# Sliding-window attention of the prompt: the value product as fp32r matmuls on high and low parts

## The chip, the cores and the metric

The kernel runs on one core of a Trainium2 chip. The metric is the device time of one execution in microseconds; before the change it is 1694.12 us, the median of three runs (1693.13 to 1695.23).

Five engines of the core run their own in-order instruction streams: TensorE (PE in the profile; its weight loads are shown apart as PEld), VectorE (DVE), ScalarE (ACT), GpSimd (POOL) and SyncE (SP), whose queue starts most of the DMA transfers here. Matmuls read SBUF and write PSUM; PSUM is then read out by DVE or ACT.

## The reference

One inference step of a two-layer decoder for a prompt of 512 tokens and 8 samples of 4 tokens, all in fp32. The change touches one piece of the first layer, the attention of the prompt over a sliding window of 128 tokens, with 16 query heads that share 4 key and value heads (4 queries to one):

```python
def gqa_attend(q, k, v, mask=None, bias=None, sink=None):
    s = jnp.einsum('...qkgd,...skd->...kgqs', q, k) * (q.shape[-1] ** -0.5)
    s = jnp.where(mask, s, NEG_INF)
    p = jax.nn.softmax(jnp.concatenate([s, sk], axis=-1), axis=-1)[..., :-1]   # sk: one sink logit per head
    return jnp.einsum('...kgqs,...skd->...qkgd', p, v)

def swa_prompt(q, k, v, sink):
    # blocks of 128 queries; each sees its own block of keys and the one before it
    o = gqa_attend(qb, with_prev(kb), with_prev(vb), mask=mask[:, None, None], sink=sink)
```

The last line of `gqa_attend` is the value product: probabilities times values.

## The kernel before

The step is one long program. Nearly all of PE's time goes to linear layers: weights arrive in pieces of 128 x 1024 numbers (`wpiece`, L154), are split by ACT into a high part that fp32r holds exactly (L162) and by DVE into the rest (L163), and each product is three fp32r matmuls, high x high, high x low, low x high (`acc3`, L180). A piece serves 48 matmuls of 256 or 288 columns. The raw weights have two buffers and the split ones three, so a DMA of a piece waits for the split two pieces earlier, and that split for the matmuls of the piece three before it.

In the first layer (`even`, L614) the program computes keys and values, four pieces of the query projection, and then runs the attention of the prompt beside the linear layers that don't depend on it: four more query pieces (L667), eight pieces of the gate `z` (L669) and twelve pieces of the convolution's input (`conv`, L723). The attention is written inside `with self.ahead(m0)` (L670), which gives it a priority as if it stood ahead of those layers. The order of every engine's stream is then worked out by a scheduler when the program is built: it fills each gap of the attention with linear matmuls. On the chip each engine runs its stream as it stands.

`swa_prompt` (L484) handles one half of the heads (`m`), a block of 128 queries (`c`), and in it two key heads (`r`) with two pairs of query heads (`i`). For one pair: scores on PE from split queries and keys into PSUM (`sc`, two buffers), a maximum on DVE (L502), exponentials on ACT (L507), the reciprocal of the sum on DVE (L510), the scaling on POOL (L513), transposes on PE (L515, by `tr`, L141) into PSUM (`tp`, two buffers), and a copy of them into the tile `PT` (L516, on DVE for the first pair and ACT for the second). When all four pairs of a block are in `PT`, the value product follows (L517 to L523): one key block (`kb`) and one key head (`r`) at a time, a stationary operand of 64 columns (the values) and 512 streamed columns (the four heads' probabilities), both in fp32. The two key heads write the two halves of one PSUM tile `pv` (one buffer); DVE copies it over the queries that it replaces (L523). All matmuls are issued in the helper `mm` at L138.

`swa_sample` (L562) follows, the same attention for the samples; its cached keys and values come by DMA into tiles `skT` and `svc` (L568, L569). Working tiles of 2176 columns (`H`, L122), among them `PT`, `skT`, `svc` and the halves of the queries, share one pool of 13 buffers.

Of the kernel before, what the change touches and what calls it, by code (L numbers as in the profile page):

```python
# [9 lines left out]
F32 = mybir.dt.float32  # L10
F32R = mybir.dt.float32r
# [4 lines left out]
ALU = mybir.AluOpType  # L16
# [3 lines left out]
P = 128  # L20
# [86 lines left out]
class Net:  # L107
# [364 lines left out]
    def stack_q(self, Q, q, m, tok):  # L472
# [7 lines left out]
            nc.vector.tensor_tensor(Q[b, r], src, Q[a, r].bitcast(F32), ALU.subtract)  # L480
        return Q


    def swa_prompt(self, q, K2, V, m):  # L484
        nc = self.nc
        for c in range(4):
            nk = 1 if c == 0 else 2
            W, k0 = 128 * nk, 128 * max(c - 1, 0)
            tok = slice(128 * c, 128 * c + 128)
            Q = self.stack_q(self.sw.tile([P, 1024], F32R, tag="QS", bufs=2, name=self.nm("QS")), q, m, tok)  # L490
            PT = self.H("PT")[:, 0:2048].rearrange("p (k r i t) -> p k r i t", k=2, r=2, i=4)
            for r in range(2):
                for i in (0, 2):
                    hd = 8 * m + 4 * r + i
                    sc = self.psum("sc", [P, 2, 256])
                    s = sc[:, :, 0:W]
                    self.mm(s, self.identb, self.maskb[:, 256 - W:256].unsqueeze(1).to_broadcast([P, 2, W]), True, False)
                    for e in range(2):
                        for z in range(2):
                            self.mm(sc[:, e, 0:W], Q[:, r, i + e], K2[z][:, m, r, k0:k0 + W], False, e == 1 and z == 1)  # L500
                    mx, nm, den, es, rec = (self.ty(2) for _ in range(5))
                    nc.vector.tensor_reduce(mx, s, AX.X, ALU.max, negate=True)  # L502
                    nc.vector.tensor_tensor(nm, mx, self.nsink[:, hd:hd + 2], ALU.min)
                    nc.vector.tensor_tensor(es, nm, self.par[:, V_SK + hd:V_SK + hd + 2], ALU.add)
                    pr = self.sw.tile([P, 2, 256], F32, tag="P", bufs=3, name=self.nm("pr"))
                    for e in range(2):
                        nc.scalar.activation(pr[:, e, 0:W], sc[:, e, 0:W], AF.Exp, bias=nm[:, e:e + 1], accum_out=den[:, e:e + 1])  # L507
                    nc.scalar.activation(es, es, AF.Exp)
                    nc.vector.tensor_tensor(den, den, es, ALU.add)
                    nc.vector.reciprocal(rec, den)  # L510
                    tp = self.psum("tp", [P, 2, 2, 128])
                    for e in range(2):
                        nc.gpsimd.tensor_scalar(pr[:, e, 0:W], pr[:, e, 0:W], rec[:, e:e + 1], 1.0, ALU.mult, ALU.mult)  # L513
                        for kb in range(nk):
                            self.tr(tp[:, kb, e], pr[:, e, 128 * kb:128 * kb + 128])  # L515
                    (nc.scalar.copy if i else nc.vector.tensor_copy)(PT[:, 0:nk, r, i:i + 2], tp[:, 0:nk])  # L516
            pv = self.psum("pv", [P, 4, 128])  # L517
            for kb in range(nk):
                blk = c - nk + 1 + kb
                for r in range(2):  # L520
                    g = 2 * m + r
                    self.mm(pv[64 * r:64 * r + 64], V[:, blk, 64 * g:64 * g + 64], PT[:, kb, r], kb == 0, kb == nk - 1)
            nc.vector.tensor_copy(q.half(m)[:, :, tok], pv)  # L523

    def sample_q(self, q, Qb):
        nc = self.nc
# [87 lines left out]
    def even(self, st, nxt, fill):  # L614
        nc, tc, I, O = self.nc, self.tc, self.I, self.O
        with ExitStack() as es:
            ev = es.enter_context(tc.tile_pool(name="even", bufs=1))
            kT = ev.tile([P, 2, NT], F32, name="kT")
            V = ev.tile([P, 5, 256], F32, name="V")
# [9 lines left out]
            for i, (o, w) in enumerate(TB):  # L629
                ps = self.psum("tr", [P, 288])  # L630
                for k in range(KD):
                    whi, wlo = wv[k // 4][0][:, k % 4], wv[k // 4][1][:, k % 4]
                    a, b = xh[k][:, o:o + w], xl[k][:, o:o + w]
# [18 lines left out]
            nc.sync.dma_start(O["p_swa_v"], V[:, 3])  # L652
            with tc.tile_pool(name="swa", bufs=1) as self.sw, tc.tile_pool(name="conv", bufs=1) as cv:
                K2 = self.stack_k(kT)
                self.linear(wq, range(4), KD, xh, xl, qe)

                def zevac(n, c, ps):
                    o, N = CH[c]
                    z = zs[n][:, o:o + N]
                    nc.vector.scalar_tensor_tensor(z, ps, 0.125, st["b"][:, o:o + N], ALU.mult, ALU.mult)  # L660
                    t = cv.tile([P, 572], F32, tag="cy", bufs=2, name=self.nm("zt"))[:, 0:N]
                    nc.scalar.activation(t, z, AF.Tanh, scale=4.0)
                    self.last = nc.vector.scalar_tensor_tensor(z, t, 1.0, z, ALU.add, ALU.mult)
                m0 = self.mark()
                self.take(q)
                self.take(zs)
                self.linear(wq, range(4, 8), KD, xh, xl, qe)  # L667
                qlast = self.last
                self.linear(self.pieces(I["we_z"], KD), range(8), KD, xh, xl, zevac)  # L669
                with self.ahead(m0):  # L670
                    self.swa_prompt(q, K2, V, 0)
                    self.swa_prompt(q, K2, V, 1)
                    self.swa_sample(q, kT, V, qlast)
                self.conv(st, xs, BC, craw, cv)
            nc.sync.dma_start(O["conv"], craw)
# [1168 lines left out]
```

## Time and profile before

| | |
|---|---|
| median of three runs | 1694.12 us |
| profiled execution | 1698.67 us, of which 1696.9 us span |
| granted clock of TensorE, mean | 0.99 |
| PE busy | 1645.9 us |
| DVE, ACT, POOL busy | 1184.0, 778.3, 328.3 us |
| DMA | 189.27 MB, 112 GB/s on average |

The profile is of one execution. Busy times are unions over an engine's instructions; matmuls are pipelined, so a busy PE may still be slowed by one matmul that takes long. What a matmul costs is best read from the distance between starts, not from its duration. An instruction in the program may be several in the trace: an fp32 matmul is two rows there.

### The profile page before, as it was taken

The page shows a single profiled execution, that of the slowest core. Times are in us where ns is not written, and L with a number is a line of the kernel's source. Part 1 is how long each engine was busy: PE and PEld are TensorE (multiplying, and loading weights), DVE is VectorE, ACT ScalarE, POOL GpSimd, SP SyncE. Part 2 cuts the span into 40 slices and gives each one's busy share as a digit, 9 for nine tenths or more (in the row PEclk, how much of TensorE's full clock was granted, in tenths as well). Part 3 has the DMA queues.
Part 4 walks back from the last instruction along what each step waited for, and adds up shares of the span by engine and source line. Part 5 has one row for each costly group of instructions (what it writes and reads, how often), then busy time and mean ns, then how long its engine had stood idle before and what let it go on. Part 6 is the DMA issues. An engine that isn't in the chain of part 4 may idle for free.

```text
span 1696.9 us, 32362 instructions
## 1 busy us (share of the span) xinstructions
PE 1645.9 (97%) x12720; PEld 1518.7 (89%) x12720; DVE 1184.0 (70%) x2296; ACT 778.3 (46%) x1603; POOL 328.3 (19%) x510
## 2 busy tenths in 40 slices
PE   6999999998999999999999998998999999999997
PEld 6988899886997999999999996655988999999997
DVE  7667678867766887677766567654567877777663
ACT  5255445344444544444445355544545444444444
POOL 5022312657422310000001203111223100000002
PEclk9999999999999999999999999999999999999999
DMA  5211424126533233232323334554551233223222
GB/s 185 63 55 39 145 82 132 51 91 237 207 100 125 81 113 102 89 103 88 106 75 107 127 116 125 160 174 149 181 178 59 75 113 100 94 100 106 75 68 86
DMA packets 71221, 189.27 MB, mean 112 GB/s; under 512 B 7612, under 2 KB 34012, under 8 KB 63452
## 3 DMA queue, kind: packets, MB, share of 16 engines
q1 hardware_dynamic: 69388, 184.84, 32.9%
q8 instruction: 100, 1.64, 0.4%
q10 hardware_dynamic: 1600, 1.83, 0.4%
q0 software_dynamic: 80, 0.52, 0.1%
q14 instruction: 53, 0.43, 0.1%
HBM read 172.22 MB, written 14.95 MB: 110 GB/s over the span
## 4 chain that ended last, share of the span: by engine, by line
PE 91%; DVE 3%; POOL 2%; ACT 1%; issue 1%; DMA 1%; SPq 0%; DVEq 0%; POOLq 0%; ACTq 0%
PE ps L138 66%; PE ps L1563 22%; PE ps L141 3%; POOL room L425 1%; DMA room<-wo_d 0%; POOL sq L421 0%; DVE split_t L1544 0%; ACT prt L1161 0%; DVE prt L1160 0%; DVE xs L879 0%; ACT split_t L162 0%; DMA mem<-mem 0%; DVE meml L252 0%; DVE x L1730 0%; DMA x<-x 0%
## 5 line engine op out<-in xcount | busy, mean ns | idle before, releaser
L138 PE MATMUL ps<-xh,split_t 128*128 128x288 f32 (+1 forms) x2304 | 463.8, 294 | 13.8 <-ACT split_t L162 11.8
L138 PEld LDWEIGHTS ps<-xh,split_t 128*128 128x128 f32 x2304 | 371.1, 190 | 19.8 <-ACT split_t L162 12.8
L1563 PE MATMUL ps<-xf,split_t 128*128 128x272 f32 x2592 | 348.9, 289 | 3.1 <-DVE split_t L1544 2.1
L138 PE MATMUL ps<-xl,split_t 128*128 128x256 f32 (+1 forms) x1152 | 339.1, 295 | 1.2 <-DVE xl L252 1.0
L1563 PEld LDWEIGHTS ps<-xf,split_t 128*128 128x128 f32 x2592 | 335.0, 188 | 4.4 <-DVE split_t L1544 3.0
L261 POOL TENSOR_TENSOR room<-room,sq 128x256 f32<-128x256 f32 (+1 forms) x96 | 86.4, 904 | 773.4 <-ACT sq L260 771.7
L138 PEld LDWEIGHTS ps<-xl,split_t 128*128 128x128 f32 x1152 | 218.9, 190 | 6.9 <-issue 4.3
L138 PE MATMUL ps<-hh,fs 128*128 128x256 f32 (+1 forms) x1024 | 206.3, 288 | 0.0
L162 ACT CAST split_t<-room 128x1024 fp32r<-128x1024 f32 (+1 forms) x128 | 130.3, 1019 | 156.5 <-PE ps L138 112.3
L163 DVE TENSOR_TENSOR split_t<-room,split_t 128x1024 fp32r<-128x1024 f32 (+1 forms) x128 | 157.0, 1229 | 31.5 <-ACT split_t L162 31.0
L138 PEld LDWEIGHTS ps<-hh,fs 128*128 128x128 f32 x1024 | 164.9, 188 | 0.4 <-ACT fs L1607 0.4
L1544 DVE TENSOR_TENSOR split_t<-fr,split_t 128x1024 fp32r<-128x1024 f32 x108 | 131.7, 1221 | 35.3 <-ACT split_t L1543 35.0
L1543 ACT CAST split_t<-fr 128x1024 fp32r<-128x1024 f32 x108 | 113.4, 1052 | 89.6 <-PE ps L1563 53.4
L138 PE MATMUL ps<-hl,fs 128*128 128x256 f32 (+1 forms) x512 | 147.3, 288 | 0.0
L138 PE MATMUL ps<-oh,split_t 128*128 128x288 f32 (+1 forms) x512 | 105.7, 298 | 1.3 <-ACT oh L246 1.2
L138 PEld LDWEIGHTS ps<-hl,fs 128*128 128x128 f32 x512 | 96.4, 188 | 0.0
L138 PEld LDWEIGHTS ps<-oh,split_t 128*128 128x128 f32 x512 | 83.2, 192 | 8.3 <-issue 5.0
L138 PE MATMUL ps<-ol,split_t 128*128 128x288 f32 (+1 forms) x256 | 77.1, 301 | 0.3 <-DVE ol L249 0.2
L1607 ACT CAST fs<-room 128x512 fp32r<-128x512 f32 x64 | 39.4, 618 | 82.6 <-PE ps L138 68.3
L252 DVE SCALAR_TENSOR_TENSOR xl<-x,room,xh 128x256 fp32r<-128x256 f32 (+1 forms) x96 | 69.6, 755 | 5.6 <-ACT xh L251 5.6
L138 PE MATMUL ps<-hh,split_t 128*128 128x256 f32 (+1 forms) x384 | 73.4, 288 | 0.0
L1620 DVE TENSOR_TENSOR x<-x,ps 128x256 f32<-128x256 f32 (+1 forms) x128 | 54.4, 433 | 26.9 <-PE ps L138 26.7
(423 smaller groups left out, 3091.2 us busy)
## 6 DMA issues: line engine op xcount, KB each, us to landing
fr<-wfi SPq DMA_DIRECT2D x36, 1024.0 KB
room<-wfo SPq DMA_DIRECT2D x64, 256.0 KB
room<-wo_e SPq DMA_DIRECT2D x16, 512.0 KB
xk<-mem_k SPq DMA_DIRECT2D x8, 1024.0 KB
xv<-mem_v SPq DMA_DIRECT2D x8, 1024.0 KB
room<-wfi SPq DMA_DIRECT2D x16, 512.0 KB
fox_k<-fox_k SPq DMA_DIRECT2D x64, 128.0 KB
fox_v<-fox_v SPq DMA_DIRECT2D x64, 128.0 KB
```

The costliest lines, as they stand in the source:

```text
L138: self.nc.tensor.matmul(out, lhsT, rhs, start=start, stop=stop)
L141: self.nc.tensor.transpose(out, in_, self.ident[0:k, 0:k])
L162: nc.scalar.copy(hi[:, 0:n], raw[:, 0:n])
L163: nc.vector.tensor_tensor(lo[:, 0:n], raw[:, 0:n], hi[:, 0:n].bitcast(F32), ALU.subtract)
L252: return nc.vector.scalar_tensor_tensor(ll, src, g, hh.bitcast(F32), ALU.mult, ALU.subtract)
L261: nc.gpsimd.tensor_tensor(acc, acc, sq[:, 0:N], ALU.add)
L425: nc.gpsimd.tensor_tensor(acc, acc, sq, ALU.add)
L1543: nc.scalar.copy(hi, t)
L1544: nc.vector.tensor_tensor(lo, t, hi.bitcast(F32), ALU.subtract)
L1563: self.nc.tensor.matmul(ps, w[a][:, k], x[:, b, k], start=start and k == 0 and i == 0, stop=k == 3 and i == 2, skip_group_check=True)
L1607: nc.scalar.copy(hi, raw)
L1620: nc.vector.tensor_tensor(x, x, ps, ALU.add)
```

## The change

The value product is computed from high and low parts, as the linear layers are, but with other operands side by side. `stack_v` makes, once, a tile `Vs` in which each key head's values of a block take 128 columns: high part and low part (for `r` = 0 high then low, for `r` = 1 the other way round). `turned` replaces the copy of the transposes by two operations: ACT writes the high part of the probabilities, DVE subtracts it from PSUM and writes the low part. `values` then runs, for one key head, two matmuls for each key block (high and low probabilities) with 128 stationary columns and 512 streamed ones, all accumulating into one PSUM tile, whose one half holds the sum over high values and whose other half the sum over low ones; ACT copies one half to the queries' place and DVE adds the other. `PT` now belongs to one key head, not to two, and the value product runs for each key head as soon as its two pairs are there.

```diff
--- before.py
+++ after.py
@@ -480,6 +480,33 @@
             nc.vector.tensor_tensor(Q[b, r], src, Q[a, r].bitcast(F32), ALU.subtract)
         return Q
 
+    def stack_v(self, V, t):
+
+        nc = self.nc
+        t = t.rearrange("p (b m r s x) -> p b m r s x", b=4, m=2, r=2, s=2)
+        src = V.rearrange("p b (m r x) -> p b m r x", m=2, r=2)
+        for r in range(2):
+            nc.scalar.copy(t[:, :, :, r, r], src[:, :, :, r])
+            nc.vector.tensor_tensor(t[:, :, :, r, 1 - r], src[:, :, :, r], t[:, :, :, r, r].bitcast(F32), ALU.subtract)
+        return t.rearrange("p b m r s x -> p b m r (s x)")
+
+    def turned(self, PT, tp):
+
+        self.nc.scalar.copy(PT[0], tp)
+        self.nc.vector.tensor_tensor(PT[1], tp, PT[0].bitcast(F32), ALU.subtract)
+
+    def values(self, q, V2, PT, r, blocks):
+
+        nc = self.nc
+        pv = self.psum("pv", [P, 4, 128])
+        n = len(blocks)
+        for j, v in enumerate(blocks):
+            for z in range(2):
+                self.mm(pv, v[:, r], PT[z][j], j == 0 and z == 0, j == n - 1 and z == 1)
+        a, b = slice(64 * r, 64 * r + 64), slice(64 - 64 * r, 128 - 64 * r)
+        nc.scalar.copy(q[a], pv[b])
+        return nc.vector.tensor_tensor(q[a], pv[a], q[a], ALU.add)
+
 
     def swa_prompt(self, q, K2, V, m):
         nc = self.nc
@@ -488,8 +515,8 @@
             W, k0 = 128 * nk, 128 * max(c - 1, 0)
             tok = slice(128 * c, 128 * c + 128)
             Q = self.stack_q(self.sw.tile([P, 1024], F32R, tag="QS", bufs=2, name=self.nm("QS")), q, m, tok)
-            PT = self.H("PT")[:, 0:2048].rearrange("p (k r i t) -> p k r i t", k=2, r=2, i=4)
             for r in range(2):
+                PT = self.H("PT", F32R)[:, 0:2048].rearrange("p (z k i t) -> p z k i t", z=2, k=2, i=4)
                 for i in (0, 2):
                     hd = 8 * m + 4 * r + i
                     sc = self.psum("sc", [P, 2, 256])
@@ -513,14 +540,9 @@
                         nc.gpsimd.tensor_scalar(pr[:, e, 0:W], pr[:, e, 0:W], rec[:, e:e + 1], 1.0, ALU.mult, ALU.mult)
                         for kb in range(nk):
                             self.tr(tp[:, kb, e], pr[:, e, 128 * kb:128 * kb + 128])
-                    (nc.scalar.copy if i else nc.vector.tensor_copy)(PT[:, 0:nk, r, i:i + 2], tp[:, 0:nk])
-            pv = self.psum("pv", [P, 4, 128])
-            for kb in range(nk):
-                blk = c - nk + 1 + kb
-                for r in range(2):
-                    g = 2 * m + r
-                    self.mm(pv[64 * r:64 * r + 64], V[:, blk, 64 * g:64 * g + 64], PT[:, kb, r], kb == 0, kb == nk - 1)
-            nc.vector.tensor_copy(q.half(m)[:, :, tok], pv)
+                    self.turned([PT[:, z, 0:nk, i:i + 2] for z in range(2)], tp[:, 0:nk])
+                self.values(q.half(m)[:, :, tok], V, [[PT[:, z, k] for k in range(nk)] for z in range(2)], r,
+                            [V[:, c - nk + 1 + k, m] for k in range(nk)])
 
     def sample_q(self, q, Qb):
         nc = self.nc
@@ -652,6 +674,7 @@
             nc.sync.dma_start(O["p_swa_v"], V[:, 3])
             with tc.tile_pool(name="swa", bufs=1) as self.sw, tc.tile_pool(name="conv", bufs=1) as cv:
                 K2 = self.stack_k(kT)
+                V2 = self.stack_v(V[:, 0:4], self.H("Vs", F32R)[:, 0:2048])
                 self.linear(wq, range(4), KD, xh, xl, qe)
 
                 def zevac(n, c, ps):
@@ -668,8 +691,8 @@
                 qlast = self.last
                 self.linear(self.pieces(I["we_z"], KD), range(8), KD, xh, xl, zevac)
                 with self.ahead(m0):
-                    self.swa_prompt(q, K2, V, 0)
-                    self.swa_prompt(q, K2, V, 1)
+                    self.swa_prompt(q, K2, V2, 0)
+                    self.swa_prompt(q, K2, V2, 1)
                     self.swa_sample(q, kT, V, qlast)
                 self.conv(st, xs, BC, craw, cv)
             nc.sync.dma_start(O["conv"], craw)
```

The order of the streams moves with it. On PE, second block of queries of the first half (`c` = 1, `m` = 0), the value products of the kernel before (`ps_1661` is `pv`, `PT_1548` the probabilities; `xh`, `xl` with `split_t` are linear matmuls):

```order
L138 MATMUL ps_1729<-kh_484,QS_1667 128x256
L141 MATMUL ps_1693<-room,pr_1687 128x128 x2
L138 MATMUL ps_915<-xh_95,split_t 128x288
L141 MATMUL ps_1693<-room,pr_1687 128x128
L138 MATMUL ps_1661<-PT_1548,V 64x512 x3
L141 MATMUL ps_1693<-room,pr_1687 128x128
```

and the same block, first key head, in the changed one (`ps_1623` is `pv`):

```order
L138 MATMUL ps_1623<-PT_1564,Vs_494 128x512
L138 MATMUL ps_1702<-kh_484,QS_1696 128x256
L138 MATMUL ps_920<-xh_80,split_t 128x288
L138 MATMUL ps_1702<-kl_485,QS_1696 128x256
...
L138 MATMUL ps_920<-xl_96,split_t 128x288
L138 MATMUL ps_1623<-PT_1564,Vs_494 128x512 x3
L138 MATMUL ps_920<-xh_95,split_t 128x288 x2
```

Before, the block's four products (two key blocks, two key heads) are one alone and three in a row; the program has ten alone and six such threes. Now each key head has its own four (two for the first block), the first of them apart from the others by linear matmuls. Between the first score matmul and the last value product stand 624 linear matmuls before and 723 in the changed program, counted in the two orders.

On DVE, where the first block's value product of the kernel before is read out (`ps_1539` is `pv`, L516 the copy into `PT`, here the second block's):

```order
L502 TENSOR_REDUCE ty_1583<-ps_1577 128x2
L456 SCALAR_TENSOR_TENSOR q_715<-ps_805,room 128x288
L503 TENSOR_TENSOR ty_1584<-ty_1583,room 128x2
L163 TENSOR_TENSOR split_t<-room,split_t 128x1024
L504 TENSOR_TENSOR ty_1586<-ty_1584,room 128x2
L516 COPY PT_1548<-ps_1569 128x2x256
L509 TENSOR_TENSOR ty_1585<-ty_1585,ty_1586 128x2
L510 RECIPROCAL ty_1587<-ty_1585 128x2
L523 COPY q_522<-ps_1539 128x4x128
```

and the same place in the changed one (its L496 is the subtraction in `turned`, L508 the addition in `values`, L529 to L537 the former L502 to L510):

```order
L529 TENSOR_REDUCE ty_1637<-ps_1631 128x2
L496 TENSOR_TENSOR PT_1564<-ps_1585,PT_1564 128x2x256
L530 TENSOR_TENSOR ty_1638<-ty_1637,room 128x2
L531 TENSOR_TENSOR ty_1640<-ty_1638,room 128x2
L508 TENSOR_TENSOR q_527<-ps_1554,q_527 64x4x128
L456 SCALAR_TENSOR_TENSOR q_720<-ps_865,room 128x288
L536 TENSOR_TENSOR ty_1639<-ty_1639,ty_1640 128x2
L537 RECIPROCAL ty_1641<-ty_1639 128x2
```

The subtraction now stands between the maximum of a pair of heads and what follows it, for every pair; before, DVE had such a copy for every second pair.

On SP, the load of the samples' cached keys and values among the weights of the convolution's input (`we_x`), before with -, now with +:

```order
+L158 DMA room<-we_x 128x1024 x7
+L590 DMA skT_2506<-swa_k 128x8x128 x2
+L591 DMA svc_2507<-swa_v 128x2048
+L594 DMA o_s_swa_k<-skT_2506 128x8x128 x2
+L158 DMA room<-we_x 128x1024
+L597 DMA o_s_swa_v<-svc_2507 124x8x256
 L158 DMA room<-we_x 128x1024 x4
-L568 DMA skT_2401<-swa_k 128x8x128 x2
-L569 DMA svc_2402<-swa_v 128x2048
```

The keys now follow seven pieces of `we_x` where they followed four. On PE the first matmul that needs them stands behind 1023 linear matmuls of the first layer, counted from the program's start, where it stood behind 913; the second piece of `we_x` ends at 960 in this count.

## Rows read from the trace of the kernel before

**Rows 1.** The page: part 1 and the shares of part 4 (share, by engine).
```profile
PE 1645.9 (97%) x12720; PEld 1518.7 (89%) x12720; DVE 1184.0 (70%) x2296; ACT 778.3 (46%) x1603; POOL 328.3 (19%) x510
PE 91%; DVE 3%; POOL 2%; ACT 1%; issue 1%; DMA 1%; SPq 0%; DVEq 0%; POOLq 0%; ACTq 0%
```

**Rows 2.** Chain of waits, 60 to 300 us: shares by line; then start, us, what.
```profile
by line: PE ps L138 93.4%; PE ps L141 6.6%
...
232.51 56.52 PE ps L138 x450
```

**Rows 3.** Busy time by stretch (columns in the first row).
```profile
core 0: us, PE busy (x) PEld busy (x) DVE busy (x) ACT busy (x) POOL busy (x), PEclk, DMA share, GB/s
75.00:213.00 138.00, 138.00 (x1009) 115.92 (x1008) 94.80 (x259) 68.75 (x219) 39.05 (x77) 1.00 0.27 82
300.00:410.00 110.00, 101.47 (x738) 83.31 (x738) 77.46 (x146) 46.61 (x104) 71.73 (x82) 0.95 0.34 116
```

**Rows 4.** Tile PT: duration ns min/median/max, starts; last row: time waited, times.
```profile
L138 PE MATMUL ps<-PT,V x56: 592/592/644, 86.0 to 212.1; 128*64 128x512 f32 x56
...
  PE ps L138: 0.7, 2
```

**Rows 5.** PE in order of time: start, us, what; one value product alone (x2).
```profile
85.64 0.43 PE L138 MATMUL ps<-xh,split_t 128*128 128x288 f32 x2
86.00 1.07 PE L138 MATMUL ps<-PT,V 128*64 128x512 f32 x2
87.00 0.40 PE L138 MATMUL ps<-xl,split_t 128*128 128x288 f32 x1
87.25 0.30 PE L138 MATMUL ps<-xh,split_t 128*128 128x288 f32 x1
```

**Rows 6.** PE in order of time: three value products in a row (x6).
```profile
210.59 0.28 PE L138 MATMUL ps<-xh,split_t 128*128 128x256 f32 x1
210.80 1.93 PE L138 MATMUL ps<-PT,V 128*64 128x512 f32 x6
212.66 0.39 PE L138 MATMUL ps<-xh,split_t 128*128 128x256 f32 x1
212.89 0.28 PE L138 MATMUL ps<-xl,split_t 128*128 128x256 f32 x1
```

**Rows 7.** PE in order of time, 415 us: full-width matmuls of 512 columns, operands fp32r.
```profile
415.90 0.84 PE L138 MATMUL ps<-split_t,memh 128*128 128x512 f32 x3
416.58 0.39 PE L138 MATMUL ps<-split_t,meml 128*128 128x512 f32 x1
```

**Rows 8.** Groups of 70 to 230 us: busy us, mean ns, idle before, releaser.
```profile
L516 DVE COPY PT<-ps 128x512 f32<-128x512 f32 x12 | 8.2, 685 | 0.8 <-PE ps L141 0.7
L523 DVE COPY q<-ps 128x512 f32<-128x512 f32 x8 | 5.5, 690 | 7.2 <-PE ps L138 7.1
L588 DVE TENSOR_TENSOR swk<-ps,room 128x512 f32<-128x512 f32 x1 | 0.7, 691 | 1.0 <-PE ps L138 1.0
L516 ACT COPY PT<-ps 128x512 f32<-128x512 f32 x12 | 7.0, 584 | 11.1 <-PE ps L141 10.9
```

**Rows 9.** Waits of 70 to 230 us: us in total, times, longest.
```profile
DVE ty L509 <- ACT ty L508: 8.8, 11, 1.9
```

**Rows 10.** SP's DMA queue in order of time, 188 us.
```profile
188.16 1.05 SPq L568 DMA_DIRECT2D skT<-swa_k  x2
...
194.38 0.38 SPq L572 DMA_DIRECT2D o_s_swa_k<-skT  x1
```

**Rows 11.** DVE in order of time: one piece of the convolution's input projection to the next.
```profile
246.06 0.43 DVE L740 TENSOR_TENSOR pad<-ps,room 128x256 f32<-128x256 f32 x1 [1.02 <-PE ps L138]
...
252.09 0.42 DVE L740 TENSOR_TENSOR pad<-ps,room 128x256 f32<-128x256 f32 x1 [1.01 <-PE ps L138]
```

**Rows 12.** The page, part 5: the two halves of splitting a weight piece.
```profile
L162 ACT CAST split_t<-room 128x1024 fp32r<-128x1024 f32 (+1 forms) x128 | 130.3, 1019 | 156.5 <-PE ps L138 112.3
...
L163 DVE TENSOR_TENSOR split_t<-room,split_t 128x1024 fp32r<-128x1024 f32 (+1 forms) x128 | 157.0, 1229 | 31.5 <-ACT split_t L162 31.0
```

## The prediction

> **What bounds the kernel now.** I read the page's busy shares first: PE is busy for 1645.9 us of the span, DVE for 70% of it, and PE holds 91% of the chain that ended last [rows 1]. Then the chain in the part of the program where the attention of the prompt runs: from 60 to 300 us it is PE alone, line after line, with no other engine in it [rows 2]. The table by stretch says the same of 75 to 213 us, from the first score matmul to the last value product: PE 138.00 of 138.00 us, DVE 94.80, ACT 68.75, TensorE at its full granted clock [rows 3]. So in this stretch a microsecond taken from PE is a microsecond of the program, as long as the other engines keep up, and work added to DVE or ACT costs nothing until PE waits for it. PE hardly does today: for everything that comes through the tile PT, in both layers, it waited 0.7 us in two places [rows 4].
>
> **What is removed.** The 28 value products are 56 rows of 512 columns in the trace [rows 4], two for each. Their durations overlap, so I take the distance between starts. A product that stands alone: from 85.64 to 87.25 us lie two rows of it and three linear matmuls [rows 5]. The long run of the chain has 450 linear matmuls in 56.52 us, 0.126 us each [rows 2]; so one product costs 1.61 - 3 x 0.126 = 1.23 us, of which about 0.2 are gaps at its two edges. Three in a row: from 210.59 to 212.89 us, less two linear matmuls, 2.30 - 0.25 = 2.05 us [rows 6]. Ten stand alone and six times three in a row: 10 x 1.23 + 6 x 2.05 = 24.6 us.
>
> In a row of three, a product takes 0.62 us (1.86 / 3), alone 1.00: the two key heads write different halves of the partitions, and neighbours of different halves overlap. The Trainium skill (TensorE: Matmul & The Clock Gate, Part 3: Packing small matmuls — row/col tiling) says that small matmuls whose outputs lie in distinct column groups run concurrently. That speaks against the change, which gives this overlap up: by the rule all 28 would cost 28 x 0.62 = 17.4 us and there would be only 4.7 us to win. The trace agrees where neighbours meet and shows ten products without one, so the sum stays with the starts as they were measured.
>
> **What is added on PE.** 56 matmuls of 512 columns with 128 stationary columns, operands fp32r. The same shape stands at 415 us, three starts in 0.68 us, 0.227 us each [rows 7]: 56 x 0.227 = 12.7 us. I charge no edges, since stationary width and type are those of the linear neighbours. If each of the 32 places where such matmuls now begin cost the 0.23 us of today's edges, it would be 7.4 us more, and that is the upper end. PE: 12.7 - 24.6 = -11.9 us.
>
> **What is added beside PE.** DVE gets 16 more operations on the transposes (32 subtractions for 16 copies) and 16 additions for 8 copies. A two-operand operation out of PSUM of this size took 691 ns once, the copies 685 and 690 [rows 8], so all count 0.69 us: 24 x 0.69 = 16.6 us more. (Eight of the subtractions, those of the first block, are half as long; this is a bound from above.) ACT gets 16 more copies of transposes and 16 copies of products, 32 x 0.584 = 18.7 us more [rows 8]. The stretch has 43.2 us of DVE and 69 us of ACT to spare [rows 3]. The two ACT and two DVE operations of the stacked values come once, before the attention, where PE has linear work; I cost them at nothing, and without that cover at 2 x 0.584 + 2 x 0.69 = 2.5 us.
>
> **The added waits.** The first matmul of a product now needs ACT's copy of the last transposes, the later ones DVE's subtraction behind it, where one copy did before. Behind a waiting matmul stands all of PE's stream, the linear layers too. Bounds: nothing (0.7 us was waited in all, for this and another use of the tile), and the whole of a copy and a subtraction, 1.27 us, for each of 16 products, 20 us. The order on PE leaves time: the 99 more linear matmuls stand between the pieces of the attention, 12.4 us over 16 products. I take a value near the low end, 0.12 us a product, 1.9 us.
>
> The samples' keys are the other new wait. SP issues their load behind the seventh piece of the convolution's input, that piece's load waits for the split of the fifth, and that for the matmuls of the second. From there a cast and a split (1.02 and 1.23 us [rows 12]) and a landing of at most 6.2 us (188.16 to 194.38 [rows 10]) make 8.5 us. PE has 63 linear matmuls (7.9 us) and four value matmuls (0.9 us) to do before it needs them: 8.8 us, just enough. From 0 to 3 us, if a landing takes half as long again; I take 0.5.
>
> **The sum.** -11.9 + 1.9 + 0.5 = -9.5 us. The profiled execution took 1698.67 us, 4.55 above the median of the runs, and I take the difference over: 1694.12 - 9.5 = 1684.6 us.
>
> **The rivals.**
>
> DVE becomes the bound (slower). It would need 94.8 + 16.6 us in the stretch, and since two pieces of the convolution (99 linear matmuls are two pieces of 48) now fall into it, two times 6.03 - 1.01 = 5.0 us more [rows 11]: 121.4 us. PE's part becomes 138 - 11.9 + 12.4 = 138.5 us. So DVE may be idle for 17 us; today it is for 43.2 [rows 3]. What it idles beyond that PE waits, and the change loses from 17 + 11.9 = 29 us on, two thirds of today's idle time. For it: the chain of one pair of heads goes back and forth between engines, DVE waited 8.8 us for ACT's small exponentials alone [rows 9], ACT gets longer too, and a subtraction now stands between a maximum and what follows it in DVE's order. Against it: much of the idle time is DVE waiting for PE (7.2 us before the copy of the products alone [rows 8]), and that shrinks where DVE has more to do. With five sixths of the idle time kept, 36 us, it is 19 - 11.9 = 7 us slower, 1701 us. Of this the Trainium skill warns (TensorEngine Tiling (Array Packing), PSUM Bottleneck): a faster TensorE leaves the reading of PSUM as it is, which may then be the limit. No row of before can show it.
>
> The waits eat the gain (no change). Every one of the 16 products waits 0.58 us, one ACT copy [rows 8], before its matmuls: 9.3 us, and 11.9 - 9.3 = 2.6 us remain, 1691.5 us. For it: ACT copies were themselves waiting for transposes before, so the product follows them closely; against it: 99 linear matmuls were put in between.
>
> It is given back later (no change). From 300 to 410 us PE is idle for 110 - 101.5 = 8.5 us [rows 3], in the state-space part, where loads and stores on SP also change places. Doubled, it would leave 1.0 us: 1693.1 us. Gone, it would be 1676.1. PE's idle time there hangs on the order of the same instructions, and nothing that the change adds runs there, so neither has much weight.
>
> **Chances.** What this kernel's measurement can tell from no change is about 0.2%, 3.4 us. The forecast with its own range, waits of 0 to 7 us (1682.2 to 1689.2 us), 0.64; the waits eat the gain, 0.15; DVE the bound, 0.11; given back later, 0.06; the later idle time gone too, 0.04. Faster: 0.64 + 0.04 = 0.68; within 0.2%: 0.15 + 0.06 = 0.21; slower 0.11. The range of 1681 to 1694 us holds the forecast, the waits that eat the gain and the giving back, and leaves out DVE as the bound and the lucky later part, 0.15.
>
> **What would show it.** In the profile of the changed kernel, the value products' 56 rows have starts 0.23 us apart where neighbours are, with no gap at their edges; the stretch from the first score matmul to the last value product takes about 141 us with 723 linear matmuls in it; PE stays near full in it, and its waits for ACT copies, DVE subtractions and the load of the samples' keys add up to some 2 us. DVE is at about 87% there. The prediction is wrong if PE's idle time in the stretch exceeds 8 us, if the products' rows stand further apart than 0.3 us, or if the part from 300 to 410 us, moved by the gain, takes longer than before.

## The result and the profile after

The changed kernel takes 1675.61 us (median of four runs, 1674.17 to 1679.51) against 1694.26 for the kernel before: a ratio of 0.9899, 95% interval 0.9881 to 0.9918. It is 18.65 us faster. The prediction had 1684.6 us and a range from 1681: the sign was right, the gain was twice what was forecast, and the time lies below the range.

The page of the changed kernel, part 1:

```profile
PE 1627.3 (97%) x12720; PEld 1518.5 (91%) x12720; DVE 1196.5 (71%) x2322; ACT 795.1 (47%) x1637; POOL 333.5 (20%) x510
```

Against [rows 1] PE is busy 18.6 us less, in a span of 1677.7 us instead of 1696.9. So nearly all of the gain is busy time of PE, and the change was forecast to take only about 12 us of work from it. The rest must be sought elsewhere.

To find it I cut both traces at the same matmuls: the 289th linear matmul on `xh` and `xl` counted from the start (in the query projection, just before the first score matmul), the 1201st (in the convolution's input, behind the attention) and the 1601st (in the output projection behind the state-space part). Between the first two lies the attention with 912 linear matmuls, between the last two the state-space part. Busy time by stretch, columns as in [rows 3]; first the kernel before:

```profile
72.67:251.89 179.22, 179.22 (x1380) 155.37 (x1378) 126.33 (x318) 84.74 (x246) 45.10 (x97) 1.00 0.26 81
251.89:456.88 204.99, 196.46 (x1427) 172.44 (x1425) 158.76 (x302) 91.37 (x185) 106.65 (x123) 0.96 0.42 143
```

and the changed one:

```profile
73.60:240.71 167.11, 167.11 (x1379) 159.65 (x1378) 137.79 (x342) 101.03 (x278) 47.30 (x97) 1.00 0.28 87
240.71:437.80 197.09, 191.04 (x1426) 168.43 (x1425) 158.81 (x302) 90.98 (x186) 107.91 (x123) 0.98 0.43 149
```

The attention is 12.1 us shorter, with PE busy throughout in both. The state-space part, in which no instruction was added or removed, is 7.9 us shorter. Two columns of its rows say by what: PE is idle for 197.09 - 191.04 = 6.05 us instead of 8.53, and the mean granted clock is 0.98 instead of 0.96. At 0.96, 0.04 x 205 = 8.2 us are lost to the lower of the clock's two levels (1.2 instead of 2.4 GHz, called half clock below); at 0.98 it is 3.9 us. Both are good to about 1 us, since the clock has two digits.

In the attention the new products look as forecast. The tile PT in the changed kernel (durations min/median/max) and a group of three products on PE:

```profile
L138 PE MATMUL ps<-PT,Vs x56: 387/395/504, 87.2 to 213.8; 128*128 128x512 f32 x56
L495 ACT CAST PT<-ps x32: 359/586/590, 82.8 to 210.7; 128x512 fp32r<-128x512 f32 x24, 128x256 fp32r<-128x256 f32 x8
L496 DVE TENSOR_TENSOR PT<-ps,PT x32: 409/683/693, 83.4 to 211.3; 128x512 fp32r<-128x512 f32 x24, 128x256 fp32r<-128x256 f32 x8
...
  PE ps L138: 0.7, 2
```

```profile
205.22 0.42 PE L138 MATMUL ps<-xh,split_t 128*128 128x288 f32 x2
205.48 0.86 PE L138 MATMUL ps<-PT,Vs 128*128 128x512 f32 x3
206.18 0.29 PE L138 MATMUL ps<-xl,split_t 128*128 128x288 f32 x1
```

Three starts in 0.70 us, with no gap at either side; one fp32 product alone took 1.61 us together with three linear matmuls [rows 5]. The last row of PT is word for word that of before [rows 4]: the 0.7 us waited there belong to the second layer, and no product of the first waited at all.

### The profile page after: what moved, and what is told of

It is laid out like the page before. It is cut to its first block, busy times and chain, and to the rows that moved or that the text cites. A ratio compares the mean times of both kernels' runs of the same rounds, so it can differ in the third digit from the quotient of the medians.

```text
span 1677.7 us, 32465 instructions
## 1 busy us (share of the span) xinstructions
PE 1627.3 (97%) x12720; PEld 1518.5 (91%) x12720; DVE 1196.5 (71%) x2322; ACT 795.1 (47%) x1637; POOL 333.5 (20%) x510
## 4 chain that ended last, share of the span: by engine, by line
PE 89%; DVE 4%; POOL 2%; issue 1%; DMA 1%; ACT 1%; DVEq 0%; SPq 0%; POOLq 0%; ACTq 0%
PE ps L138 64%; PE ps L1586 22%; PE ps L141 3%; POOL room L425 1%; DMA vr<-wd_v 0%; ACT prt L1184 0%; DMA o_s_ssm<-hb 0%; DVE meml L252 0%; DMA room<-wo_d 0%; DVE xs L902 0%; ACT split_t L162 0%; POOL sq L421 0%; DVE split_t L1567 0%; POOL E L862 0%; DVE prt L1183 0%
## 5 line engine op out<-in xcount | busy, mean ns | idle before, releaser
L138 PEld LDWEIGHTS ps<-xh,split_t 128*128 128x128 f32 x2304 | 370.7, 190 | 17.0 <-ACT split_t L162 12.7
```

Of the source, the lines that this page charges most:

```text
L138: self.nc.tensor.matmul(out, lhsT, rhs, start=start, stop=stop)
```

## The experiments

Many of them hold the order of the streams fixed in a part of the program, so that one thing alone changes there. That is done by ordering edges for the scheduler, which make no engine wait on another; the order itself is a table of numbers:

```python
for prev, i in zip(names, names[1:]):     # one engine's instructions, in the order wanted
    tc.add_manual_dep(by[i], prev, mybir.DependencyInfo(mybir.DependencyClass.NoSync, mybir.DependencyReason.SCHED_ONLY), reason="order")
```

The summary: the median, the ratio to the kernel before run on the same chip, and from each profile the attention, the state-space part with PE's idle time in it, and whose order it has there (all cut as above).

| run | us | ratio, 95% interval | attention | state-space (PE idle) | order there |
|---|---|---|---|---|---|
| before | 1694.26 | | 179.2 | 205.0 (8.5) | before |
| changed | 1675.61 | 0.9899 [0.9881, 0.9918] | 167.1 | 197.1 (6.1) | changed |
| after_again | 1677.51 | 0.9895 [0.9875, 0.9915] | 167.2 | 196.4 (5.1) | changed |
| b_late | 1687.74 | 0.9954 [0.9935, 0.9972] | 179.7 | 197.7 (4.6) | changed |
| a_late | 1682.18 | 0.9925 [0.9905, 0.9946] | 167.6 | 202.3 (10.0) | before |
| b_move | 1694.70 | 1.0005 [0.9993, 1.0018] | 179.2 | 202.1 (8.8) | before, one place on PE |
| b_eb | 1690.85 | 0.9982 [0.9971, 0.9992] | 179.2 | 201.1 (8.0) | before, one place on DVE |
| b_adj | 1683.84 | 0.9945 [0.9926, 0.9965] | 169.8 | 201.5 (7.5) | before |
| b_adj_late | 1678.28 | 0.9900 [0.9884, 0.9917] | 170.1 | 196.4 (5.1) | changed |
| a_dve2 | 1689.75 | 0.9971 [0.9960, 0.9983] | 179.1 | 197.3 (6.2) | changed |
| a_act2 | 1682.92 | 0.9931 [0.9916, 0.9946] | 168.0 | 197.5 (4.6) | changed |
| a_z0 | 1669.84 | 0.9856 [0.9837, 0.9874] | 162.7 | 197.5 (4.6) | changed |
| best | 1670.57 | 0.9859 [0.9840, 0.9878] | 167.1 | 197.4 (4.6) | changed |
| best2 | 1672.53 | 0.9872 [0.9854, 0.9889] | 170.1 | 198.4 (5.3) | changed |

**b_late and a_late: the two halves of the change apart.** The edit of each is the table of the other kernel's order, from the convolution's input to the end of the first layer, on all five engines.

```diff
         Net(nc, tc, ctx, I, O).run()
+        late_order(nc, tc)
```

> The kernel before with its own attention; from the convolution's input to the first layer's end every engine's stream is put in the order that the changed kernel has there (same instructions). Theory A, the later part won by its new order: the time falls by about 7.6 us (2.5 us of idle time and 5.1 us of lower granted clock between 300 and 440 us, from the two profiles), to about 1686.7 us, and the granted clock stays full at 339 us. Theory B, the later part won because the attention ended earlier or because of one lucky profile: 1694.3 us, no change.

> The changed kernel with the new attention; from the convolution's input to the first layer's end every stream in the order of the kernel before. Theory A (order): it loses 7.6 us of its 18.7 and stands at about 1683.2 us, with a stretch of half clock near 330 us. Theory B (not the order): 1675.6 us, as the changed kernel. The attention's own part is the same in both: 11 us less than before at the end of the convolution's input on PE.

Theory A holds in both. The order alone, with the old attention, is 6.8 us faster (1687.74 against 1694.52 in those runs; by the interval 4.7 to 11.0 us); the new attention with the old order keeps 12.3 us. Together that is 19.1 us, where the whole change gained 18.7 (17.0 in after_again, beside these two runs). The table does not reach the later layers, which the scheduler ordered anew in b_late; there the time behind the 1601st matmul is 1239.5 us against 1240.0 before, so the gain is not made there. The state-space part's row by stretch, first of b_late, then of a_late:

```profile
249.71:447.38 197.67, 193.05 (x1427) 170.90 (x1426) 159.23 (x303) 90.93 (x186) 103.33 (x123) 0.97 0.43 149
```

```profile
241.34:443.60 202.26, 192.22 (x1427) 169.44 (x1426) 165.34 (x309) 92.43 (x188) 109.56 (x125) 0.97 0.44 148
```

PE's idle time goes with the order: 4.6 us here, 10.0 there. The clock goes with it only in part (0.97 in both). Over all the profiles of the table the part takes 196.4 to 198.4 us in the changed kernel's order, with 4.6 to 6.2 us of idle time on PE, and 201.1 to 205.0 in the order of before, with 7.5 to 10.0, whatever the attention is.

**after_again: the changed kernel once more.**

> The changed kernel once more, for a second profile: 1675.6 us. If the clock follows from the order, its stretches of half clock after 60 us fall in the same places as in the first profile (380 and 414 us, one stretch of 3.4 us each); if it is chance, elsewhere.

The stretches of half clock fell at 378 and 412 us, each 3.4 us long, as in the first profile (380 and 414 us). The places recur: all nine profiles with the changed kernel's order have two such stretches at these two places of the part. Their length does not recur: it is 3.4 us in four of them and 6.8 us in five, b_late among these. The first place in the changed kernel and in b_late (columns as above, the clock is the third from the end):

```profile
379.00:385.00 6.00, 5.12 (x30) 5.12 (x31) 6.00 (x8) 0.95 (x4) 5.53 (x8) 0.72 0.76 274
```

```profile
387.00:395.00 8.00, 6.86 (x36) 6.86 (x36) 7.01 (x8) 2.62 (x9) 7.31 (x9) 0.57 0.68 253
```

So at this place 1.7 us are lost in the one and 3.4 in the other, by the same order; what decides between them is not shown.

**b_move and b_eb: one wait in the state-space part.** In the profile of before the longest wait of this part that isn't for a transfer or a norm is this one on PE:

```profile
336.26 0.28 PE L138 MATMUL ps<-ol,split_t 128*128 128x256 f32 x1
338.75 0.42 PE L138 MATMUL ps<-cs,ohs 128*128 128x128 f32 x1 [2.22 <-DVE eb L859]
```

and just behind it the granted clock drops (the window from 340 us, columns as above; 0.72 is the mean over its 10 us):

```profile
340.00:350.00 10.00, 10.00 (x60) 8.48 (x57) 4.76 (x15) 3.50 (x9) 4.75 (x4) 0.72 0.01 2
```

In b_move the 17 linear matmuls behind the waiting one go ahead of it (the numbers are those of the table of PE's order):

```diff
-... 1726 1379 1310-1313 1380-1382 1404 1406 1408 1410 1417 1727 1754-1769 ...
+... 1726 1727 1754-1769 1379 1310-1313 1380-1382 1404 1406 1408 1410 1417 ...
```

> The kernel before, every stream in its own order, but for one place on PE in the state-space part: 17 linear matmuls of the output projection that stood behind the matmul that waits at 338.75 us (the one with 2.22 us of idle time ahead of it) now stand ahead of it, as in the changed kernel's order. Theory A, this wait is the main thing that the new order mended: 2.2 us less idle time, and with it the half-clock stretch behind it (6.8 us long, 3.4 us lost) gone or shorter; 1694.5 - 2.2 to 5.6, about 1690.5 us. Rival: the wait only moves to the next place, or the gain sat in the order as a whole: 1694.5 us.

The rival was right: no change, ratio 1.0005. PE in b_move at that place:

```profile
334.76 0.27 PE L138 MATMUL ps<-oh,split_t 128*128 128x256 f32 x1
337.13 0.40 PE L138 MATMUL ps<-oh,split_t 128*128 128x288 f32 x1 [2.10 <-DVE eb L859]
```

The linear matmuls moved there wait for the same product `eb`. So it isn't a matter of what PE has at hand but of when DVE comes to `eb`. DVE in the kernel before:

```profile
330.53 2.20 DVE L163 TENSOR_TENSOR split_t<-room,split_t 128x1024 fp32r<-128x1024 f32 x1
332.65 0.68 DVE L819 TENSOR_TENSOR xdt<-ps,dt 128x512 f32<-128x512 f32 x1
333.90 4.20 DVE L879 SCALAR_TENSOR_TENSOR xs<-zs,xs 128x256 f32<-128x256 f32 x4 [0.57 <-POOL xs L861]
338.02 0.68 DVE L859 TENSOR_TENSOR eb<-eb,ps 128x512 f32<-128x512 f32 x1
```

Four operations of the gate, which nobody on PE waits for at that time, stand ahead of `eb`, which PE waits for. b_eb turns that round on DVE:

```diff
-L879 SCALAR_TENSOR_TENSOR xs<-zs,xs 128x256 x4
 L859 TENSOR_TENSOR eb<-eb,ps 128x512
 L868 TENSOR_TENSOR hst<-hst,ps 128x512
+L879 SCALAR_TENSOR_TENSOR xs<-zs,xs 128x256 x4
```

> The kernel before, every stream in its own order, but for one place on DVE in the state-space part: the product eb (L859) and the addition to the state (L868) that stood behind four operations of the gate (L879, 4.2 us, themselves behind a POOL operation) now stand ahead of them. PE's 2.2 us wait was for this eb, also in b_move, where the matmuls put in between waited for it too. Theory: eb ends at about 334 us, before PE comes to it at 336.5 us; the 2.2 us are gone, and the half-clock stretch behind them (1.7 to 3.4 us lost) is rarer: 1689 to 1692.3 us. Rival: the gate's operations, 1.4 us later, hold up what waits for them and the time stays at 1694.5 us.

DVE and PE in b_eb:

```profile
331.71 0.67 DVE L859 TENSOR_TENSOR eb<-eb,ps 128x512 f32<-128x512 f32 x1
333.37 0.69 DVE L868 TENSOR_TENSOR hst<-hst,ps 128x512 f32<-128x512 f32 x1 [0.99 <-POOL hst L867]
333.98 2.75 DVE L879 SCALAR_TENSOR_TENSOR xs<-zs,xs 128x256 f32<-128x256 f32 x4
```

```profile
334.84 0.22 PE L138 MATMUL ps<-cs,ohs 128*128 128x128 f32 x1
...
337.92 1.10 PE L138 MATMUL ps<-xdt,Bt 128*128 128x512 f32 x2 [0.85 <-DVE E L836]
```

The wait is gone (0.85 us come back at the next place), and two operations out of their place on one engine are worth 3.3 us (ratio 0.9982, interval 0.9971 to 0.9992, which is 1.4 to 4.9 us). The 2.2 us of the wait lie in this interval; that more than the wait was won is not shown. Nor does the profile show where it was won: over the whole part PE is idle for 8.0 us in b_eb, and for 7.5 to 10.0 in the four profiles that have the wait. (b_eb's profile is of one of the slowest of its twelve executions, 1693.95 us, b_move's of the fastest, 1689.86.) The half-clock stretch behind the wait comes and goes: of the four profiles with this wait, those of before and a_late have one behind it (6.8 and 3.4 us long), those of b_adj and b_move none, and so the expectation for b_move was wrong on that too. The changed kernel's order has at the corresponding place a wait of 0.57 us:

```profile
329.83 1.10 PE L138 MATMUL ps<-xdt,Bt 128*128 128x512 f32 x2 [0.57 <-DVE eb L882]
```

By the medians, 3.3 of 6.8 us, about half of what b_late gained is this wait and what follows from it; the two intervals are too wide to hold that firmly. The rest I did not separate.

**b_adj: the fp32 product with the key heads alternating.** What speaks against the change, tried by itself in the order of before: the same fp32 products in one run per block, neighbours always in different halves.

```diff
-                for r in range(2):
+                for r in (1, 0):
                     g = 2 * m + r
-                    self.mm(pv[64 * r:64 * r + 64], V[...], PT[:, kb, r], kb == 0, kb == nk - 1)
+                    one = self.mm(pv[64 * r:64 * r + 64], V[...], PT[:, kb, r], kb == 0, kb == nk - 1)
+                    if kb == 0 and r:
+                        first = one
+                    else:
+                        self.after(one, first)
```

> The kernel before, fp32, with the value products of a block issued in one run, the two key heads taking turns (two or four in a row, never one alone); the rest of the first layer in the order of before. If neighbours of different halves overlap throughout: a run of four costs 0.2 + 4 x 0.62 = 2.7 us, one of two 1.4 us, 6 x 2.7 + 2 x 1.4 = 19.0 us against 24.6, so 5.6 us less than before, about 1688.7 us. If the overlap in the runs of three was a matter of the last two only, or if the whole run now waits for the last copy: within 2 us of before.

It gained 10.7 us, twice the expectation. A run of four on PE (eight rows):

```profile
203.93 0.40 PE L138 MATMUL ps<-xh,split_t 128*128 128x256 f32 x2
204.25 1.94 PE L138 MATMUL ps<-PT,V 128*64 128x512 f32 x8
206.12 0.39 PE L138 MATMUL ps<-xl,split_t 128*128 128x256 f32 x1
```

From 203.93 to 206.12, less two linear matmuls, are 1.94 us for four products; three took 2.05 in [rows 6]. A pair of opposite halves costs what one costs alone: the 28 products now take 14.0 us by the distances between their neighbours' starts, 22.8 in the kernel before and 13.6 as fp32r in the changed one, all read in the same way. That is 8.8 of the 9.4 us by which the attention is shorter; the scheduler moved the transposes too, by up to 18 linear matmuls. The 0.62 us a product that I read from a row of three counted its unpaired third in.

**b_adj_late: both, without the fp32r product.**

> b_adj (fp32 products, the two key heads alternating in one run) with the rest of the first layer in the changed kernel's order. If the two gains add: b_adj's 1683.8 us less the 6.8 us of b_late, 1677 us, the changed kernel's time without its extra work on DVE and ACT. If the two share a cause: 1682 us or more.

1678.28 us, 15.9 below the kernel before, where 10.7 and 6.8 make 17.5: the gains add, within the intervals, and the mere reordering comes as far as the changed kernel did (ratio 0.9900 against 0.9899 and 0.9895, the same within their intervals).

**a_dve2, a_act2, a_z0: how close the next bound is.** Each has the rest of the first layer, from the convolution's input on, in the changed kernel's order. The attention itself is not held: the scheduler laid its streams out anew in each of the three, and the later layers a little differently too. So they are read by the attention, and with its order in mind.

```diff
-        self.nc.vector.tensor_tensor(PT[1], tp, PT[0].bitcast(F32), ALU.subtract)
+        for _ in range(2):
+            self.nc.vector.tensor_tensor(PT[1], tp, PT[0].bitcast(F32), ALU.subtract)
```

> The changed kernel with each of the 32 subtractions on the transposes done twice (the second writes the same numbers); the rest of the first layer in the changed kernel's order. DVE gets 24 x 0.69 + 8 x 0.41 = 19.8 us more in the attention and stands at 131 of 138 us. Theory A (PE alone bounds, DVE's idle time can be used): the attention stays at 167 us between the same two linear matmuls, 1675.6 us. Theory B (the rival of DVE as the bound was near): PE waits for the subtractions, 5 to 13 us more, 1681 to 1689 us.

The attention is 12.0 us longer, the time 14, as theory B had it, but the run does not show theory B's cause. The stretch of a_dve2, whole and then in two parts, the first up to PE's first idle time:

```profile
70.08:249.14 179.06, 172.21 (x1381) 161.90 (x1381) 151.15 (x372) 101.48 (x276) 42.96 (x97) 0.98 0.26 78
70.08:206.97 136.89, 136.89 (x1055) 132.34 (x1054) 114.75 (x291) 81.30 (x229) 31.95 (x64) 1.00 0.21 64
206.97:227.80 20.83, 13.98 (x131) 10.71 (x131) 16.15 (x39) 10.03 (x31) 5.66 (x15) 0.92 0.52 161
```

and PE's longest waits in it:

```profile
PE ps L138 <- DVE PT L497: 2.4, 2, 1.7
PE ps L141 <- ACT swk L617: 1.4, 1, 1.4
PE ps L141 <- DVE PT L497: 1.0, 1, 1.0
```

For 136.89 us DVE is busy for 84% of the time, 82% in the changed kernel, and PE waits for nothing. All of PE's 6.85 us of idle time lies in the 20.83 us behind, with a loss of clock besides, and there DVE is busy for 78%. What differs there is the order: among the last four value products the scheduler put 24 linear matmuls, in the changed kernel 150 (counted in the two traces). With little else in its stream PE waits for the chain, 3.4 us of it for the doubled subtractions. DVE's busy time in the whole stretch grew by 13.4 us, not by 19.8, since the times of neighbouring operations overlap and two of the convolution's fell out of the stretch. So longer work on DVE can cost the gain, but whether DVE's time or the order that came with it costs the 12.0 us is not separated.

a_act2 does the same to ACT's copy (`for _ in range(2)` around `nc.scalar.copy(PT[0], tp)`).

> The changed kernel with ACT's 32 copies of the transposes done twice (the second writes the same numbers); the rest of the first layer in the changed kernel's order. ACT gets 24 x 0.58 + 8 x 0.36 = 16.8 us more and stands at 105 of 138 us, and each subtraction and product comes 0.58 us later after the transposes. Theory A (in a_dve2 it was DVE's time that ran out, not the length of the chain): 0 to 3 us more, 1676 to 1679 us. Theory B (the length of the chain decides): about as much as a_dve2, 10 us more or over, 1686 us.

The attention is 0.8 us longer and PE waits for nothing in it, so theory A's time holds there: the chain between transposes and product may be 0.58 us longer, in an order with 137 linear matmuls among the last four products. That DVE's time is what is scarce does not follow. The median of 1682.92 is above what theory A expected all the same: the stretch behind the 1601st matmul took 5.4 us more in its profile than in the changed kernel's, in later layers that the edit doesn't touch but the scheduler ordered a little differently, and I have no cause for it.

a_z0 leaves out the low part of the probabilities in the product:

```diff
-            for z in range(2):
-                self.mm(pv, v[:, r], PT[z][j], j == 0 and z == 0, j == n - 1 and z == 1)
+            self.mm(pv, v[:, r], PT[0][j], j == 0, j == n - 1)
```

> The changed kernel without the matmuls of the low part of the probabilities (28 of the 56 matmuls of the value product are left out; the low part is still computed); the rest of the first layer in the changed kernel's order. If PE bounds the attention: 28 x 0.227 to 0.243 = 6.4 to 6.8 us less there, about 1669 us. If the other engines' chain has become as long as PE's: the attention stays near 167 us and the time near 1675.6 us.

1669.84 us, but of the 6.6 us taken from PE (13.6 to 7.0 by the starts) only 4.4 appear in the attention, and PE is idle for 1.0 us in it. The attention's order is another here too, and the rest is not separated. So most of what is taken from PE still comes out as time: PE bounds the changed kernel's attention.

**best and best2: a faster kernel.** The second layer's attention has the same fp32 product. In best the changed kernel gets the edit of b_adj there, in best2 b_adj_late does.

> The changed kernel, and in the second layer's attention of the prompt, which still has the fp32 product with the two key heads in the two halves, the neighbours are made to alternate halves and stand in one run, as in the earlier run b_adj. There the 40 products (80 rows) take 29.8 us by the distances of starts, 11 of them alone at 1.08 us. In pairs at 0.98 us (b_adj) they take 19.6 us: about 10 us less, 1666 us. If the run now waits for the last copy of its transposes: less of it, down to nothing, 1675.6 us.

> b_adj_late, and the second layer's products alternating too (as in the run best): fp32 throughout, no extra work on DVE or ACT. Where the changed kernel gained 5 to 7 us by this edit, here the same: 1677 - 6 = 1671 us. If PE's waits in the second layer grow by the runs that wait for the last copy: 1674 us or more.

best takes 1670.57 us, 5 to 7 less than the changed kernel (1675.61 and 1677.51), not 10: the 40 products went from 29.9 to 23.1 us, since two of the runs stand in a stretch of half clock or wait (16 rows took 5.5 us at one place and 3.7 at another). best2, with no more work on DVE or ACT than before, takes 1672.53, between its two expectations. The intervals of the two overlap: with the second layer's products paired as well, fp32 in a better order still comes as far as the fp32r product.

## Why the prediction was wrong

**The step that failed** is the one on the later part, "PE's idle time there hangs on the order of the same instructions, and nothing that the change adds runs there, so neither has much weight". The first half is true and was the reason to give it weight: the order was different, it stood in both programs to be read, and it was worth 6.8 us by itself (b_late). I gave the case that some of that time is won 0.04. Nor did I count the clock: [rows 3] had 0.95 for the granted clock there, which at 110 us is 5.5 us, beside 8.5 us of idle time, and I priced the idle time alone. The rival "it is given back later" had the right place and the wrong sign. None of the three signs by which the prediction was to be wrong came up: PE is not idle in the attention, the products' starts are 0.23 us apart, and the later part is shorter, not longer. All three look for a loss, so they could not show a second gain.

**The value products.** Forecast 24.6 us removed and 12.7 added; measured 22.8 and 13.6, so 9.2 us instead of 11.9. My two estimates for a product alone and three in a row (1.23 and 2.05 us) were each single places; the medians are 1.10 and 1.95. Another 2.9 us came beside them: the transposes take 1.7 us less by their starts, the samples' scores 0.6. I take it that they have cheaper neighbours now; no run separates it. The attention as a whole gained 12.1 us, beside the 11.9 forecast for PE. That the sum fits is luck: its two terms are off by 1.8 and 0.9 us, and a gain that was not forecast made up for it.

**The waits** of 1.9 and 0.5 us did not come. PE is busy for 167.11 of 167.11 us, and the samples' keys were there in time: the load was issued at 204.5 us and the first matmul that needs them started at 211.2.

```profile
L138 PE MATMUL ps<-skT,Qb x32: 272/273/297, 211.2 to 212.9; 128*32 128x128 f32 x32
L590 SPq DMA_DIRECT2D skT<-swa_k x2: 385/478/570, 204.5 to 204.9; - x2
```

**DVE as the bound.** It did not become one. The rival's rule was that DVE's idle time stays; between the two cuts it fell from 179.22 - 126.33 = 52.9 us to 167.11 - 137.79 = 29.3, as the prediction's reason against this rival expected, and PE waited for nothing. How much more DVE could take is not shown: in a_dve2 the attention took 179.1 us and all of its gain was gone, but in another order. The Trainium skill warns (TensorEngine Tiling (Array Packing), PSUM Bottleneck) that reading PSUM stays as it is when TensorE gets faster, and may then be the limit. In the changed kernel it was not, and a_dve2, where reading took longer, does not show such a limit apart from the order.

**The overlap that the change gives up** was worth more than I priced. Paired throughout, the 28 fp32 products cost 14.0 us (b_adj), not 17.4, and against that the fp32r form is 0.4 us shorter on the products themselves and 2.7 us on the attention (167.1 against 169.8). Most of what the change won there it won because the old products stood unpaired. The Trainium skill's rule (TensorE: Matmul & The Clock Gate, Part 3: Packing small matmuls — row/col tiling), that small matmuls in distinct column groups run concurrently, agrees with the rows: 1.94 us for four, 1.10 for one alone.

## What to carry to other kernels

When a scheduler lays out the streams, a change moves the order of instructions that it doesn't touch; compare the two orders for the part behind the change too, and price its idle time and its clock from the rows of before, in both directions. Before replacing a half-wide matmul by a wider one with more work on other engines, look whether its neighbours alternate between the halves: two edits of order (b_adj, b_eb) here gave 10.7 and 3.3 us with no instruction added. Doubling an operation tells an engine's margin only where the order is held as well: in a_dve2 the linear matmuls moved too, and PE's idle time stood where they were missing.

## What the runs showed of the hardware that was not expected

A pair of fp32 products in opposite halves costs no more than one (1.10 us alone, 1.94 for two pairs): one alone leaves half of its time to a neighbour, and an order that puts a linear matmul there throws it away.

DVE and POOL took longer where certain operations of theirs met. In the kernel before, the split of a weight piece on DVE (330.53 us, above) took 2.20 us, 1.23 in the mean [rows 12]; it began while this POOL operation ran, and the next one of POOL, which began while the split ran, took 2.26 us, where the changed kernel has 1.29 at 312.21 us:

```profile
330.36 1.29 POOL L839 TENSOR_TENSOR E<-E,CBm 128x512 f32<-128x512 f32 x1
331.61 2.26 POOL L861 TENSOR_TENSOR xs<-xs,eb 128x512 f32<-128x512 f32 x1
```

Of the four gate operations (4.20 us in the kernel before, 2.75 in b_eb) those that began beside a POOL operation, three before and two in b_eb, each ended 0.27 to 0.29 us behind its end; the others, with POOL idle, took 0.41 us. So the late `eb`, and with it PE's wait, came in part, by these rows, from where POOL's operations happened to fall. DVE's products with one operand in PSUM (`xdt` and, in b_eb, `eb`) took their usual 0.68 and 0.67 us beside a POOL operation. The Trainium skill (GPSIMD Engine Reference, 1. Specifications) names contention with VectorE instructions that have two SBUF inputs, which the split and the gate operations are. The rows agree with it; no run here took the POOL operations away to show it.
